# A two-block transformer forward pass on one core: the first transfers reordered, the first sum of squares taken by products with ones, idle products added, two small operations moved

## The chip, the core and the metric

The kernel runs on one core of one Trainium2 chip. The core has a matrix engine (TensorE, PE in the profile, with its weight loads listed as PEld), a vector engine (VectorE, DVE), a scalar engine (ScalarE, ACT), GpSimd (POOL) and SyncE (SP), which here issues all transfers; 16 DMA engines carry them. The metric is the device time of one execution in microseconds, as the median of several runs.

## The reference, cut to what matters

Two transformer blocks follow each other on 256 tokens of width 1024, all in fp32. What the change touches stands at the very start of the first:

```python
c_act = jax.nn.silu(c)
mod = c_act @ mod_w[layer] + mod_b[layer]
sh1, sc1, g1, sh2, sc2, g2 = jnp.split(mod, N_MOD, axis=-1)
u = modulate(rms_norm(h, norm_mix[layer]), sh1, sc1)   # x * (1 + scale) + shift
q, z_f, v, g = jnp.split(u @ a_w_in, ...)              # HGRN2 mixer, then gate, FFN
sm = softmax(a_lb, axis=0); lower_bounds = cumsum(sm, axis=0) - sm[0]
f = lb + (1 - lb) * sigmoid(z_f); k = (1 - lb) * (1 - sigmoid(z_f))
```

Behind that come the recurrence, a feed-forward layer, a banded attention layer with its own feed-forward layer, and the second block: sliding-window attention beside spatial gating, cross attention to a memory, and a mixture of 32 experts.

## The kernel before, in words

Activations are kept transposed: 1024 features as 8 chunks (k) of 128 partitions, 256 tokens along the free dimension; `h` holds the input. A matrix product in fp32 quality is done by three products in a faster format: each operand is split into a high part (`whi`, `uh`, made by ScalarE) and a remainder (`wlo`, `ul`, made by VectorE), and `mm3` (L197 to L200) issues high x high, high x low and low x high.

The start runs as follows. SyncE issues `crow` (the condition vector, 4 KB), the input `h` in four parts of 256 KB, and `cols` (107.5 KB: gains, biases and other column constants). ScalarE squares the four parts (L356), VectorE adds the squares to `sqs` (L358), and one pair of products with a matrix of ones (L486) sums over the partitions. `inv_rms` (L287 to L296) turns that sum into `r`: a logarithm and an identity on ScalarE, an exponential, and three operations on VectorE. Meanwhile `crow` is spread over the partitions by two products with ones (L362) and passed through silu into `cb`.

The modulation of the first norm is taken chunk by chunk, in `u_row(k)` (L500). Two tiles of 128 x 1024 modulation weights are each multiplied with `cb` and summed along the row by VectorE in `mod_row` (L368): g = 0 gives the shift, g = 1 the scale. Two small ScalarE operations (L512, L513) put bias and gain to them, VectorE makes `ut` from `h`, the scale and `r` (L516), ScalarE the high part `uh` (L517), VectorE the remainder `ul` (L521). `gb` (L490) is a product of `cols` columns that L513 reads. `w_split` (L524) splits a 128 x 512 piece of the weights `a_w_in`. The loop at L537 goes over 32 pieces, four for each chunk k; each step first issues, by the letters of `ROW_SEQ`, the next steps of `u_row(k + 1)` (r) and of the split three pieces ahead (s), then 12 matmuls: 48 for each chunk, in 8 chunks.

After that loop come the sigmoids of the forget gate (`f_out`, L582), operations with the lower bound (`lbt`, `lb`, `omlb`, `nomlb`; L552 to L562) and the next weights, split at L193 and L194.

What sets the order: the engines run their own queues in order. The order within a queue is chosen at build time by a planner that goes by data and by its own estimates; it may move an instruction ahead of others. `keep(...)` (tc.keep_in_program_order) pins an instruction behind the one that stands before it in the program on its engine. So in both kernels the first `mod_row` is pinned behind `gb`, and each `keep` after it behind the last one. Transfers are issued in the order of the program as far as their buffers are free: the weight buffers (`wslot`, tag "w") are six, the buffers of `whi` and `wlo` four each. `table()` loads the table set of logarithm and exponential on ScalarE; other sets are loaded where an operation needs one that isn't there.

Of the kernel before, what the change touches and what calls it, by code (L numbers as in the profile page):

```python
# [93 lines left out]
def _build(ctx, tc, nc, A, out, dbg):  # L94
# [20 lines left out]
    nc.sync.dma_start(crow, A["rows"][:, ROWS["c"][0]:ROWS["c"][0] + D])  # L115
    for i in range(4):
        nc.sync.dma_start(h[:, 2 * i:2 * i + 2, :], A["xT"][i * 256:i * 256 + 256].rearrange("(k p) t -> p k t", p=P))
    cols = cp.tile([P, NCOL], F32, name="cols")
    nc.sync.dma_start(cols, A["cols"])
    ident = cp.tile([P, P], F32, name="ident")  # L120
# [16 lines left out]
    def colblk(name):  # L137
        o, w = COLS[name]
        return cols[:, o:o + w]
# [17 lines left out]
    def uid(s):  # L157
        ctr[0] += 1
        return f"{s}{ctr[0]}"
# [188 lines left out]
    def hpair(kk):  # L348
        return h[:, 2 * kk:2 * kk + 2, :]
# [3 lines left out]
    sqs = gp.tile([P, 2, T], F32, tag="sq", name="sqs", bufs=2)  # L353
    for kk in range(4):
        sq = gp.tile([P, 2, T], F32, tag="whi", name=uid("sq"), bufs=4) if kk else sqs
        nc.scalar.activation(sq, hpair(kk), AF.Square)  # L356
        if kk:
            nc.vector.tensor_add(sqs, sqs, sq)  # L358
    cb = sp.tile([P, D], F32, name="cb")
    for i in range(2):  # L360
        ps = bank(pa).rearrange("p a b -> p (a b)")
        nc.tensor.matmul(ps, ones[0:1, :], crow[:, i * 512:i * 512 + 512], start=True, stop=True)  # L362
        nc.scalar.activation(cb[:, i * 512:i * 512 + 512], ps, AF.Silu)
# [119 lines left out]
    table()  # L483
    ss = pm.tile([P, T], F32, tag="mm", name=uid("ss"))
    for k2 in range(2):
        nc.tensor.matmul(ss, ones, sqs[:, k2, :], start=k2 == 0, stop=k2 == 1)  # L486
    r = inv_rms(ss, D)
# [8 lines left out]
    keep = tc.keep_in_program_order  # L496
# [3 lines left out]
    def u_row(k):  # L500

        wm = wslot(D)
        for g in range(2):
            nc.sync.dma_start(wm[:, g, :], A["modT"][g, k * P:k * P + P, :])
        ws[k] = wslot(2048)
        nc.sync.dma_start(ws[k][:, 0, :], A["a_w_in"][k * P:k * P + P, 0:2048])
        one = slice(k, k + 1)
        mod_row(wm[:, 0, :], 0, k, keep)
        yield
        mod_row(wm[:, 1, :], 1, k, keep)  # L510
# [39 lines left out]
    with tc.tile_pool(name="hgrn", bufs=1, reuse_waits="tile") as hp:  # L550

        lbt = hp.tile([P, 3, 8], F32, name="lbt")  # L552
        nc.vector.tensor_sub(lbt[:, 0, :], colblk("lb"), colblk("lb"))
# [1110 lines left out]
```

## Time and profile before

| | before |
|---|---|
| median of 3 runs | 1345.49 us (1344.38 to 1346.59) |
| the profiled execution | 1346.06 us, span 1344.3 us |
| TensorE busy | 1221.1 us (91%) |
| VectorE busy | 719.2 us (54%) |
| ScalarE busy | 571.6 us (43%) |
| GpSimd busy | 12.1 us (1%) |
| DMA | 80.9% of the 16 engines' span, 302 GB/s of HBM traffic |

The span is the time between the first and the last thing that the profile shows; the execution's own time is 1.76 us more. A busy share is an average over the whole span, and stages differ: the dense part fills TensorE and VectorE, the mixture of experts at the end waits for its weights.

### The profile page before, as it was taken

Reading aid. Unit: us, or ns where it says so; the run is one execution under the profiler, and the core shown is the slowest. Engines: PE = TensorE matmul, PEld = TensorE weight load, DVE = VectorE, ACT = ScalarE, POOL = GpSimd, SP = SyncE. Lnnn points to the kernel's source line nnn. Section 1 sums busy time; section 2 is a strip of 40 time slices with the busy share of each in tenths; the row PEclk is TensorE's granted clock in tenths of the full one; section 3 lists DMA queues with packets and bytes.
Section 4 is the critical chain, followed back from the end, with each engine's and each line's share of the span. In section 5 each row is a group of like instructions: output and inputs, shape, how many; then the busy total and the mean of one; then the engine's idle time right before and its main releaser. Section 6 shows DMA issues by size and latency. Waiting matters only on the chain.

```text
span 1344.3 us, 23689 instructions
## 1 busy us (share of the span) xinstructions
PE 1221.1 (91%) x9336; PEld 934.7 (70%) x9336; DVE 719.2 (54%) x1549; ACT 571.6 (43%) x1179; POOL 12.1 (1%) x36
## 2 busy tenths in 40 slices
PE   7999899999999999999999989999778776778795
PEld 5967899999979789999999889974223132222222
DVE  7999899888798877555568877631000000000000
ACT  5755664555575656555567767531101011000100
POOL 2000000000000000000000000000000000000000
PEclk9999999999999999999999989999898899888899
DMA  9958799999979649555235246889999999999998
GB/s 364 382 185 307 260 339 325 329 318 354 331 253 326 215 162 298 199 184 185 93 110 189 95 162 233 318 321 421 421 421 421 421 421 421 421 420 422 417 409 274
DMA packets 152566, 408.13 MB, mean 304 GB/s; under 512 B 11265, under 2 KB 79105, under 8 KB 129922
## 3 DMA queue, kind: packets, MB, share of 16 engines
q1 hardware_dynamic: 152450, 406.56, 80.9%
q8 instruction: 75, 1.23, 0.4%
q14 instruction: 41, 0.34, 0.1%
HBM read 403.38 MB, written 3.15 MB: 302 GB/s over the span
## 4 chain that ended last, share of the span: by engine, by line
PE 54%; DMA 33%; DVE 8%; ACT 2%; SPq 1%; issue 1%; POOL 0%; DVEq 0%; ACTq 0%
DMA w<-in_w 30%; PE acc L200 9%; PE acc L199 9%; PE acc L198 8%; PE ps L200 7%; PE ps L199 7%; PE ps L198 7%; DVE wlo L194 2%; DMA mt<-in_modT 1%; DVE mt L368 1%; PE ss L324 1%; PE r L1450 1%; DVE ut L335 1%; DMA w<-in_ffn_w_in 1%; SPq L1437 1%
## 5 line engine op out<-in xcount | busy, mean ns | idle before, releaser
L193 ACT ACTIVATE whi<-w 128x512 fp32r<-128x512 f32 (+1 forms) x448 | 278.5, 627 | 237.8 <-PE ps L199 110.0
L194 DVE TENSOR_TENSOR wlo<-w,whi 128x512 fp32r<-128x512 f32 (+1 forms) x448 | 299.8, 682 | 110.7 <-ACT whi L193 109.9
L1450 PE MATMUL r<-w,xe 128*32 128x512 f32 x1024 | 186.9, 664 | 58.8 <-DMA w<-in_w 58.6
L200 PE MATMUL ps<-uh,wlo 128*128 128x256 f32 x768 | 215.6, 281 | 1.3 <-DVE wlo L194 1.3
L199 PE MATMUL ps<-ul,whi 128*128 128x256 f32 x768 | 215.7, 281 | 0.5 <-DVE ul L342 0.5
L198 PE MATMUL ps<-uh,whi 128*128 128x256 f32 x768 | 215.6, 281 | 0.0
L1467 DVE SCALAR_TENSOR_TENSOR hs<-r,sc,hs 128x512 f32<-128x512 f32 (+1 forms) x9 | 6.1, 690 | 349.3 <-PE r L1450 348.9
L198 PE MATMUL acc<-uh,whi 128*128 128x256 f32 x592 | 168.7, 291 | 7.8 <-ACT uh L517 4.3
L1450 PEld LDWEIGHTS r<-w,xe 128*32 128x32 f32 x1024 | 39.6, 118 | 193.9 <-DMA w<-in_w 121.7
L200 PE MATMUL acc<-uh,wlo 128*128 128x256 f32 x592 | 167.5, 286 | 1.7 <-DVE wlo L194 1.7
L199 PE MATMUL acc<-ul,whi 128*128 128x256 f32 x592 | 168.2, 286 | 0.2 <-DVE ul L339 0.2
L200 PEld LDWEIGHTS ps<-uh,wlo 128*128 128x128 f32 x768 | 144.5, 188 | 2.1 <-DVE wlo L194 2.1
L199 PEld LDWEIGHTS ps<-ul,whi 128*128 128x128 f32 x768 | 144.6, 188 | 0.7 <-DVE ul L342 0.7
L198 PEld LDWEIGHTS ps<-uh,whi 128*128 128x128 f32 x768 | 144.6, 188 | 0.0
L368 DVE SCALAR_TENSOR_TENSOR mt<-mt,cb 128x1024 f32<-128x1024 f32 x96 | 116.8, 1219 | 11.7 <-DMA mt<-in_modT 11.7
L1496 PE MATMUL r<-w,hT 128*32 128x512 f32 (+1 forms) x544 | 94.3, 626 | 31.6 <-DMA w<-in_w 31.5
L198 PEld LDWEIGHTS acc<-uh,whi 128*128 128x128 f32 x592 | 111.8, 192 | 11.9 <-ACT uh L517 5.3
L200 PEld LDWEIGHTS acc<-uh,wlo 128*128 128x128 f32 x592 | 113.2, 192 | 3.3 <-DVE wlo L194 2.3
L199 PEld LDWEIGHTS acc<-ul,whi 128*128 128x128 f32 x592 | 113.3, 191 | 1.8 <-issue 0.8
L200 PE MATMUL acc<-hh,wlo 128*128 128x256 f32 x352 | 98.3, 279 | 0.3 <-DVE wlo L194 0.3
L198 PE MATMUL acc<-hh,whi 128*128 128x256 f32 x352 | 98.6, 280 | 0.0
L199 PE MATMUL acc<-hl,whi 128*128 128x256 f32 x352 | 98.2, 279 | 0.0
(327 smaller groups left out, 1699.8 us busy)
## 6 DMA issues: line engine op xcount, KB each, us to landing
w<-in_w SPq DMA_DIRECT2D x172, 1024.0 KB, 19.8
mt<-in_modT SPq DMA_DIRECT2D x96, 512.0 KB, 5.5
w<-in_ffn_w_in SPq DMA_DIRECT2D x88, 512.0 KB, 5.7
w<-in_ffn_w_out SPq DMA_DIRECT2D x22, 1024.0 KB, 8.5
w<-in_w SPq DMA_DIRECT2D x40, 512.0 KB, 10.2
w<-in_a_w_in SPq DMA_DIRECT2D x16, 1024.0 KB, 9.1
w<-in_modT SPq DMA_DIRECT2D x16, 512.0 KB, 8.8
w<-in_kv_w SPq DMA_DIRECT2D x8, 1024.0 KB, 6.9
```

The lines of the kernel that those rows point to most:

```text
L193: keep(nc.scalar.activation(hi, raw, AF.Copy))
L194: keep(nc.vector.tensor_sub(lo, raw, hi.bitcast(F32)))
L198: nc.tensor.matmul(o, lh, rh, start=first, stop=False, skip_group_check=True)
L199: nc.tensor.matmul(o, lh, rl, start=False, stop=False, skip_group_check=True)
L200: nc.tensor.matmul(o, ll, rh, start=False, stop=last, skip_group_check=True)
L324: nc.tensor.matmul(ss, ones, sq[:, k2, :], start=kk == min(adds, 1) and k2 == 0, stop=kk == 3 and k2 == 1)
L335: keep(nc.vector.scalar_tensor_tensor(t, src, gain, r, op0=ALU.mult, op1=ALU.mult))
L368: keep(nc.vector.scalar_tensor_tensor(w, w, 1.0, cb, op0=ALU.mult, op1=ALU.mult, accum_out=modr[:, g, j:j + 1]))
L1437: nc.sync.dma_start(ts[e][:, :, o % 512:o % 512 + o2 - o], src("w2", e)[:, o:o2].rearrange("(p c) n -> p c n", p=P))
L1450: keep(nc.tensor.matmul(hps[i][s, :], xe[k][:, s], w[nm, e, k], start=k == 0, stop=k == KC - 1))
L1467: nc.vector.scalar_tensor_tensor(hc[:, c, :], h3[:, c, :], rs, hc[:, c, :], op0=ALU.mult, op1=ALU.mult)
L1496: keep(nc.tensor.matmul(yp[s, :], hT[:, c, s], w[e, o // 512, c][:, o % 512:o % 512 + n], start=c == 0, stop=c == 3))
```

## The change

The first transfers are issued in another order: `crow`, two parts of `h`, the scale's modulation tile of chunk 0, the other two parts of `h`, the shift's tile, `cols`, and then the first row of `a_w_in` in two halves, the half that is split first ahead of the other. The tiles are allocated at the top; `u_row(0)` uses them instead of issuing its own transfers.

The squares are no longer added by VectorE. Each of the four parts is squared (three by VectorE, the last by ScalarE) and goes into the sum by two products with ones of its own. `inv_rms` is written out there with one ScalarE operation less. Between the parts stand idle products of ones with ones (2 at first, then 2, 2, 2 and 8), whose result nobody reads. The table load moves ahead of the last square. In each `u_row` the scale's row is now taken ahead of the shift's; the order of their transfers in the later chunks stays. The first operation of the lower bound is pinned behind what VectorE does before it in the program, that is, behind the last weight remainder of the loop.

```diff
     crow = sp.tile([P, D], F32, tag="mt", name="crow", bufs=3)[0:1]
     nc.sync.dma_start(crow, A["rows"][:, ROWS["c"][0]:ROWS["c"][0] + D])
+
+    wm0 = wp.tile([P, 2, D], F32, tag="w", name="wm0")
+    ws0 = wp.tile([P, 1, 2048], F32, tag="w", name="ws0")
     for i in range(4):
         nc.sync.dma_start(h[:, 2 * i:2 * i + 2, :], A["xT"][i * 256:i * 256 + 256].rearrange("(k p) t -> p k t", p=P))
+        if i % 2:
+            nc.sync.dma_start(wm0[:, 1 - i // 2, :], A["modT"][1 - i // 2, 0:P, :])
     cols = cp.tile([P, NCOL], F32, name="cols")
     nc.sync.dma_start(cols, A["cols"])
+    for i in (1, 0):
+        nc.sync.dma_start(ws0[:, 0, i * D:i * D + D], A["a_w_in"][0:P, i * D:i * D + D])
...
     table("silu_and_others")
-    sqs = gp.tile([P, 2, T], F32, tag="sq", name="sqs", bufs=2)
-    for kk in range(4):
-        sq = gp.tile([P, 2, T], F32, tag="whi", name=uid("sq"), bufs=4) if kk else sqs
-        nc.scalar.activation(sq, hpair(kk), AF.Square)
-        if kk:
-            nc.vector.tensor_add(sqs, sqs, sq)
+    keep = tc.keep_in_program_order
     cb = sp.tile([P, D], F32, name="cb")
+    ss0 = pm.tile([P, T], F32, tag="mm", name=uid("ss"))
+    idle = pb.tile([P, T], F32, tag="bg", name=uid("idle"))
+
+    def warm(n):
+
+        for _ in range(n):
+            keep(nc.tensor.matmul(idle[:, 0:P], ones, ones, start=True, stop=True))
+
+    def first_squares(kk, engine):
+        sq = gp.tile([P, 2, T], F32, tag="whi", name=uid("sq"), bufs=4)
+        if engine is nc.vector:
+            keep(nc.vector.tensor_mul(sq, hpair(kk), hpair(kk)))
+        else:
+            keep(nc.scalar.activation(sq, hpair(kk), AF.Square))
+        for k2 in range(2):
+            keep(nc.tensor.matmul(ss0, ones, sq[:, k2, :], start=kk == 0 and k2 == 0, stop=kk == 3 and k2 == 1))
+
+    warm(2)
     for i in range(2):
         ps = bank(pa).rearrange("p a b -> p (a b)")
-        nc.tensor.matmul(ps, ones[0:1, :], crow[:, i * 512:i * 512 + 512], start=True, stop=True)
-        nc.scalar.activation(cb[:, i * 512:i * 512 + 512], ps, AF.Silu)
+        keep(nc.tensor.matmul(ps, ones[0:1, :], crow[:, i * 512:i * 512 + 512], start=True, stop=True))
+        keep(nc.scalar.activation(cb[:, i * 512:i * 512 + 512], ps, AF.Silu))
+    table()
+    for kk in range(4):
+        first_squares(kk, nc.scalar if kk == 3 else nc.vector)
+        warm((2, 2, 2, 8)[kk])
...
-    table()
-    ss = pm.tile([P, T], F32, tag="mm", name=uid("ss"))
-    for k2 in range(2):
-        nc.tensor.matmul(ss, ones, sqs[:, k2, :], start=k2 == 0, stop=k2 == 1)
-    r = inv_rms(ss, D)
+
+    r, t = (gp.tile([P, T], F32, tag=f"rms_{x}256", name=uid(x), bufs=2 if x == "r" else 1) for x in "rt")
+    nc.scalar.activation(r, ss0, AF.Ln, scale=1.0 / D, bias=epsc[:, 0:1])
+    nc.scalar.activation(r, r, AF.Exp, scale=-0.5)
+    nc.vector.scalar_tensor_tensor(t, ss0, D * EPS, r, op0=ALU.add, op1=ALU.mult)
+    nc.vector.scalar_tensor_tensor(t, t, -0.5 / D, r, op0=ALU.mult, op1=ALU.mult)
+    nc.vector.scalar_tensor_tensor(r, t, 1.5, r, op0=ALU.add, op1=ALU.mult)
...
     def u_row(k):
 
-        wm = wslot(D)
-        for g in range(2):
-            nc.sync.dma_start(wm[:, g, :], A["modT"][g, k * P:k * P + P, :])
-        ws[k] = wslot(2048)
-        nc.sync.dma_start(ws[k][:, 0, :], A["a_w_in"][k * P:k * P + P, 0:2048])
+        if k:
+            wm = wslot(D)
+            for g in range(2):
+                nc.sync.dma_start(wm[:, g, :], A["modT"][g, k * P:k * P + P, :])
+            ws[k] = wslot(2048)
+            nc.sync.dma_start(ws[k][:, 0, :], A["a_w_in"][k * P:k * P + P, 0:2048])
+        else:
+            wm, ws[k] = wm0, ws0
         one = slice(k, k + 1)
+        mod_row(wm[:, 1, :], 1, k, keep)
+        yield
         mod_row(wm[:, 0, :], 0, k, keep)
-        yield
-        mod_row(wm[:, 1, :], 1, k, keep)
         yield
...
-        nc.vector.tensor_sub(lbt[:, 0, :], colblk("lb"), colblk("lb"))
+        keep(nc.vector.tensor_sub(lbt[:, 0, :], colblk("lb"), colblk("lb")))
```

## Rows read from the trace of the kernel before

**Rows 1.** Windows by stage: us, busy time and count of each engine, PEclk, DMA, GB/s

```profile
24.00:59.00 35.00, 34.91 (x295) 34.71 (x294) 34.18 (x61) 21.25 (x45) 0.00 (x0) 1.00 1.02 390
870.00:1344.00 474.00, 377.35 (x2235) 146.31 (x2233) 30.24 (x99) 52.62 (x131) 0.20 (x1) 0.93 0.98 400
```

**Rows 2.** Timeline of the start: start us, us, engine, line, operation, out<-in, count, [idle before]

```profile
2.28 3.75 PE L362 MATMUL acc<-crow,ones 1*128 1x512 f32 x4 [2.28 <-DMA crow<-in_rows]
...
9.38 0.16 DVE L490 SCALAR_TENSOR_TENSOR gb<-cols 128x8 f32<-128x8 f32 x1
...
9.52 2.07 PE L486 MATMUL ss<-sqs,ones 128*128 128x256 f32 x4 [3.50 <-DVE sqs L358]
...
9.71 1.22 DVE L368 SCALAR_TENSOR_TENSOR w<-w,cb 128x1024 f32<-128x1024 f32 x1
...
11.37 1.22 DVE L368 SCALAR_TENSOR_TENSOR w<-w,cb 128x1024 f32<-128x1024 f32 x1
...
13.48 0.63 ACT L530 ACTIVATE whi<-w 128x512 fp32r<-128x512 f32 x1 [0.19 <-DMA w<-in_a_w_in]
...
14.76 0.48 DVE L516 SCALAR_TENSOR_TENSOR ut<-h,modc,r 128x256 f32<-128x256 f32 x1
...
15.89 0.80 PE L198 MATMUL acc<-uh,whi 128*128 128x256 f32 x2 [4.29 <-ACT uh L517]
```

**Rows 3.** DMA issues at 2.66, 3.17, 3.68 and 4.16: count, KB each, us to landing

```profile
h<-in_xT SPq DMA_DIRECT2D x1, 256.0 KB, 5.3
...
cols<-in_cols SPq DMA_DIRECT2D x1, 107.5 KB, 5.1
...
w<-in_modT SPq DMA_DIRECT2D x1, 512.0 KB, 6.0
...
w<-in_modT SPq DMA_DIRECT2D x1, 512.0 KB, 6.8
```

**Rows 4.** Timeline of the first chunks of the loop, columns as in rows 2

```profile
17.01 0.41 PE L198 MATMUL acc<-uh,whi 128*128 128x256 f32 x1
17.22 0.41 PE L199 MATMUL acc<-ul,whi 128*128 128x256 f32 x1
...
21.01 0.28 PE L198 MATMUL ps<-uh,whi 128*128 128x256 f32 x1
21.12 0.28 PE L199 MATMUL ps<-ul,whi 128*128 128x256 f32 x1
...
21.63 0.28 ACT L512 ACTIVATE modc<-modr,cols 128x1 f32<-128x1 f32 x1
21.81 0.37 ACT L513 ACTIVATE modc<-modr,gb,cols 128x1 f32<-128x1 f32 x1
22.22 0.48 DVE L516 SCALAR_TENSOR_TENSOR ut<-h,modc,r 128x256 f32<-128x256 f32 x1 [1.04 <-ACT modc L513]
...
27.82 0.39 ACT L513 ACTIVATE modc<-modr,gb,cols 128x1 f32<-128x1 f32 x1 [0.24 <-DVE w L368]
28.30 0.48 DVE L516 SCALAR_TENSOR_TENSOR ut<-h,modc,r 128x256 f32<-128x256 f32 x1
```

**Rows 5.** Timeline where the loop ends and the forget gate begins

```profile
58.69 1.29 DVE L532 TENSOR_TENSOR wlo<-w,whi 128x512 fp32r<-128x512 f32 x2
59.20 1.28 ACT L582 ACT_TABLE_LOAD   x1
60.49 2.07 ACT L582 ACTIVATE f<-acc 128x512 f32<-128x512 f32 x4
...
63.39 0.68 DVE L194 TENSOR_TENSOR wlo<-w,whi 128x512 fp32r<-128x512 f32 x1
...
64.48 0.40 PE L199 MATMUL acc<-wlo,uh 128*128 128x512 f32 x1
```

**Rows 6.** Windows of 1 us in the mixture of experts, columns as in rows 1

```profile
948.00:949.00 1.00, 0.29 (x1) 0.14 (x2) 0.00 (x0) 0.00 (x0) 0.00 (x0) 1.00 1.01 418
949.00:950.00 1.00, 1.00 (x2) 0.00 (x0) 0.00 (x0) 0.00 (x0) 0.00 (x0) 0.54 1.06 442
```

More of the change, by code (lines that the diff above doesn't have):

```diff
@@ L495, in _build @@
     qps = [[bank(), bank()], [bank(), bank(pb)]]
-    keep = tc.keep_in_program_order
     ws = [None] * KC
```

## The prediction, made blind

> **What bounds the kernel now.** I read the stages first, then the start instruction by instruction, then the landings, then the loop that follows.
>
> The stages [rows 1] say what a saved microsecond is worth. From 24 to 59 us TensorE is busy 34.91 of 35 us and VectorE 34.18: both are full, and what starts earlier ends earlier. The last 474 us run at 400 GB/s with 0.98 of the DMA time used, but that stream can only begin when the dense part gives up its weight buffers. So I let a shift of the first rows reach the end undiminished; I see nothing after the start that waits for a fixed time.
>
> The start [rows 2] is a chain on VectorE. The small product `gb` runs at 9.38, after `cols` has landed; two modulation rows follow (9.71 and 11.37, 1.22 us each), then three operations for `r`, the first weight remainder and `ut` at 14.76; the first real matmul goes at 15.89. On ScalarE the first weight split stands at 13.48, after 0.19 us of waiting for its data. What set the chain going was the wire: counting its issue, `cols` landed at 3.17 + 5.1 = 8.27, modulation row 0 at 3.68 + 6.0 = 9.68 and row 1 at 4.16 + 6.8 = 10.96, and the last part of the input at 2.66 + 5.3 = 7.96 [rows 3].
>
> In the loop [rows 4] matmuls start 0.21 us apart at 17 us and 0.11 to 0.12 us apart at 21 us: 256 columns at 1.2 and at 2.4 GHz, although the granted clock prints 1.00. Some 20 matmuls from 15.89 on go at the slow level. That holds the split buffers, ScalarE waits, and VectorE sits idle 1.04 us before the second row's `ut` at 22.22.
>
> **The change, part by part.**
>
> *Transfers in another order.* The bytes are the same, so I read landings by position. Before, 1,028 KB were down at 7.96, 1,135 at 8.27, 1,647 at 9.68 and 2,159 at 10.96 [rows 3]. Now 512 KB of modulation come ahead of the third part of the input and 512 more ahead of `cols`. By interpolation the last input part (1,540 KB) lands at 9.4 instead of 8.0, the second modulation tile (2,052) at 10.7 and `cols` (2,159) at 11.0 instead of 8.3. SyncE issues these some 0.5 us apart, well ahead of the wire, so its queue costs nothing; the split weight transfer adds one issue, and the half needed first lands about 1.2 us earlier, which no row shows as the limit.
>
> *Where that hurts.* The first modulation row is kept behind `gb`, which reads `cols`. So although its own tile is there at about 8 us (1,028 KB), it can't start before about 11.1. Of the 1.66 us from one row's start to the next, about 0.5 were three small lower-bound operations, which are gone from here; the rows now take 1.15 + 1.22, from 11.1 to 13.5. From the end of the second row (11.37 + 1.22 = 12.59) to `ut` it was 2.17 us: two small operations, the split, the remainder, with the `r` operations beside them. Less the 0.19 for data that is 1.98, so `ut` at 15.4, 0.6 later than 14.76, and the three `r` operations fit beside it as before. The bounds: if `gb` is not late at all, the rows can begin at 9.7 and `ut` at 14.1, -0.7; if the `r` operations stand between the two modulation rows, +1.9 (rival three). I take +0.6, the sum in program order.
>
> *Squares into the sum.* Three additions of 0.69 on VectorE become three products of the same shape, and ScalarE loses three squares: nothing gained on VectorE. The sum is now eight fp32 products instead of two. The two at 9.52 took 2.07 us at the slow level [rows 2], about 0.86 each. TensorE is held by the `cb` products until 6.0 (2.28 + 3.75), then has 6 real and 6 idle products before the last pair. Each idle product is half as wide, 0.43. All slow, that is 5.2 + 2.6 = 7.8 us: the last pair starts at 13.8 and ends at 15.5, too late; all fast from 8 us on, the last pair waits for the last square (9.4 + 0.63) and ends near 11.3, 0.3 before the 11.59 of before. I expect 12 to 13. From the sum's end to `ut` it was 14.76 - 11.59 = 3.17 us, some of it the second modulation row and some the identity that is gone; a sum at 12.2 meets `ut` at 15.4 even at 3.17. So: 0, with bounds -0.3 and +2.0 (the sum at 15.5 and 2 us from there).
>
> *Idle products.* Up to 14 more of them, on an engine that is otherwise waiting, cost only by delaying the sum (counted). Their worth is the 1.04 us of VectorE idle time [rows 4], not the 2 us that 20 matmuls lose, because at 0.118 us TensorE would meet VectorE's chain: without the gap `ut` follows `ut` by 22.22 - 14.76 - 1.04 = 6.42. I take -1.0; bounds -2.0 (20 matmuls, 0.1 us each) and 0. The level can be lost again: at 949 us the granted clock, 1.00 until then, falls to 0.54 in a microsecond that follows one with TensorE busy only 0.29 us [rows 6], and here some 2 to 3 us lie between the last idle product and the first real one. The Trainium skill, "TensorE: Matmul & The Clock Gate" (HAM oscillation), says that an engine left idle goes back to the low rate and pays the slow start again; by it alone the gain here would be 0. The trace agrees that a sparse stretch loses the level; I leave it a one in ten rival.
>
> *Modulation rows swapped in every row.* In the loop ScalarE's two small operations come in the order L512, L513. Before, L512 was free early and only L513 waited for the second modulation row (0.24 us, at 27.82), ending 28.21; `ut` ran at 28.30 [rows 4]. Now L512 needs the second row too, and L513 follows it by 0.18 (21.63, 21.81): `ut` at about 28.43. VectorE has no slack, so +0.13 for each of rows 2 to 7 and 0.05 for row 1: +0.8. Bounds 0 (if VectorE had hidden waits to give) and +1.3 (7 times the 0.18).
>
> *The lower-bound chain moved.* `keep` puts its first subtraction behind the last remainder, which ends at 58.69 + 1.29 = 59.98 [rows 5]. ScalarE's exponential then comes at about 60.15 instead of 9.95. The table for the sigmoid is loaded at 59.20 now, while ScalarE waits for the accumulators. If the exponential goes first, that load starts at 60.35: 1.15 us later for the sigmoids at 60.49, the next weight split and its remainder on VectorE (63.39, ended 64.07). TensorE takes that remainder at 64.48, so 0.4 is hidden: +0.7. Bounds 0 and +2.4 (rival two).
>
> **Sum.** +0.6 + 0 - 1.0 + 0.8 + 0.7 = +1.1 us. The profiled execution took 1346.06 us (span 1344.3 and 1.76 around it), so its like would be 1347.2; it lies 0.6 above the median 1345.49, so I predict 1346.6.
>
> **Rivals.**
> 1. *It does what it is meant to.* `gb` isn't late and the first matmul goes 0.7 us earlier, the clock is high (-1.0 to -1.5), VectorE's swap is hidden and the exponential finds a gap: -0.7 - 1.2 = -1.9, 1343.6. For it: VectorE loses 0.5 us of small work at the start, and the 1.04 us gap is real. Against it: the landing of `cols`, and a VectorE that is full to 98% from 24 to 59.
> 2. *Slower: the exponential falls between the sigmoids.* The first sigmoid's accumulators are ready at about the time of the subtraction; if the queue has one sigmoid ahead of the exponential, ScalarE loads the exponential's table, then the sigmoid's again: 2 loads of 1.28 + 0.21 = 2.8 us, less the 0.4 hidden = 2.4 in place of 0.7. Total +2.8, 1348.3. It decides by the order on ScalarE alone. For it: the tie at 60 us; against it: the exponential comes first in the program. The Trainium skill, "ScalarE: Activation LUTs" (What ACT_TABLE_LOAD costs), adds a drain to each switch, 2.66 us in all; by that the total would be near +5.6. The trace shows the sigmoids starting 1.29 us after the load began, so the row decides.
> 3. *Slower at the start: `r` between the modulation rows.* Nothing but data orders `r` on VectorE, so it may stand ahead of the second row; the row then ends 1.3 later (1.9 - 0.6), and all behind it. Total +2.4, 1347.9. For it: `r` comes first in the program; against it: before, both rows ran ahead of `r`.
> 4. *The clock stays low or falls back.* The -1.0 is lost, which makes +2.1, and the sum of squares may come up to 2.0 later, +4.1; at +2.6, a quarter of the way, 1348.1.
>
> **Chances.** Forecast 0.42, rival one 0.22, two 0.16, three 0.10, four 0.10. A measurement of this kernel tells 0.2% (2.7 us) from no change, so faster means under 1342.8 and slower over 1348.2. Faster needs more than rival one in full, 0.06. Slower takes most of rival two, the unlucky parts of three and four, and the forecast's tail: 0.20. The same 0.74. The range reaches from a little beyond rival one to a microsecond above rival two, 1343.3 to 1349.4.
>
> **What would show it.** `gb` and the first modulation row at about 11 us and `ut` at 15.4 (right), or the modulation row at 8 to 9 us (transfers wrongly read). The first real matmuls 0.12 us apart, and `ut` to `ut` 6.4 to 6.5 us after the first row. L513 ending 0.13 closer to its `ut` in each later row, and `ut` to `ut` longer by as much. One or three table loads near 60 us. The prediction is wrong if the product at 64.48 comes more than 1 us earlier or 3 us later, or if a shift there is not found again at the end.

## The result, and the profile after

The changed kernel took 1365.64 us (median of 4 runs, 1365.24 to 1368.59), the kernel before beside it 1345.86 us: a ratio of 1.0143, 95% interval [1.0128, 1.0158], 17 to 21 us slower. The forecast was 1346.6 us, with a range up to 1349.4. The prediction was wrong in size and in kind.

The profiled execution has a span of 1366.6 us, 22.3 more than before. Where the time goes is read by following the same instruction through both traces. The table gives, for each kernel of this study, how many microseconds later than in the profiled kernel before an instruction starts, at seven places (their start times before in the head), and the span's difference. The rows below "after" belong to the experiments, which are told further down.

| kernel | 15.9 first real matmul | 57.1 last `ut` of the loop | 70.3 last `qx` product | 94.8 last `uml` | 148.4 last `ul` of the HGRN output | 205.6 first FFN output product | 450.3 first `kT,qT` product | span |
|---|---|---|---|---|---|---|---|---|
| after | +3.6 | +4.6 | +7.5 | +7.5 | +7.2 | +14.8 | +22.5 | +22.3 |
| e1 pin alone | -0.6 | -1.1 | +1.8 | +3.4 | +5.3 | +14.5 | +18.3 | +17.2 |
| e5 table loads alone | +0.1 | -0.2 | +2.4 | +4.5 | +2.6 | +9.3 | +15.1 | +14.2 |
| e6 pin, no exponential | -0.5 | -0.3 | +1.4 | +1.1 | +0.9 | +9.4 | +15.1 | +15.3 |
| e11 third order | -0.5 | -1.1 | +0.4 | +1.2 | +3.7 | +3.6 | +5.3 | +5.5 |
| e2 no pin | +3.0 | +4.0 | +4.0 | +4.0 | +4.1 | +3.3 | +3.6 | +5.2 |
| e3 no pin, no idle products | +2.1 | +2.5 | +2.5 | +2.5 | +3.8 | +3.9 | +3.4 | +2.4 |
| e9 e3 with r behind the rows | +0.8 | +1.1 | +1.1 | +1.1 | +2.4 | +2.7 | +4.2 | +4.0 |
| e4 swap alone | +1.1 | +2.0 | +2.0 | +2.0 | +1.6 | +2.6 | +1.6 | +2.6 |
| e13 transfers alone | +0.8 | +1.0 | +1.0 | +1.0 | +1.3 | +1.5 | +2.0 | +2.4 |
| e14 squares alone | +2.0 | +1.8 | +1.8 | +1.8 | +1.7 | +2.1 | +1.3 | +0.3 |
| e15 14 idle products alone | +0.6 | -0.5 | -0.4 | -0.5 | +1.8 | +2.1 | +1.9 | +0.9 |
| e10 26 idle products alone | +2.7 | +0.5 | +0.5 | +0.5 | +1.9 | +3.0 | +2.3 | +2.2 |
| e12 start mended | +2.5 | +0.3 | +0.3 | +0.3 | +0.5 | +1.2 | +2.6 | +6.1 |
| e7 rows' transfers by GpSimd | +0.2 | +0.4 | +2.0 | +1.7 | +5.7 | +12.8 | +37.2 | +36.9 |
| e8 the same with the pin | +0.1 | +0.1 | +4.5 | +4.5 | +8.3 | +14.9 | +38.8 | +39.0 |

Three cautions. The start itself moves by a few tenths to 1 us from run to run (e11 changes nothing there and shows -0.5 and -1.1). And each trace is one execution, while the kernel before ranged over 7 to 8 us in a set of runs (its medians there 1347.0 to 1347.8): differences of 1 or 2 us late in the span are spread, and totals are taken from the ratios. The profiled execution of after is the slowest of its four, 3 us above the median; those of e2 and e12 lie 2.6 and 3.0 us above theirs, those of e14, e8 and e11 3.9, 3.4 and 2.3 below. Last, TensorE's granted clock isn't the same in every execution: between 92 and 102 us it is 0.83 in e3, e9, e10 and e11 and 1.00 in before, e13 and e15. In e3, e9 and e10, which change nothing there, that stretch lies in the 1.3 to 1.4 us that they lose between 94.8 and 148.4.

The line "after" has three losses: +3.6 us at the start (+4.6 by the loop's end), +2.9 at the sigmoids, and +15 between 95 and 450 us; from there on it is 1 to 1. First the start, from the timeline of after (start, duration, engine, line, operation; in brackets the idle time before it and what ended it); it answers to [rows 2].

```profile
10.69 0.16 DVE L516 SCALAR_TENSOR_TENSOR gb<-cols 128x8 f32<-128x8 f32 x1
10.77 1.22 DVE L392 SCALAR_TENSOR_TENSOR wm<-wm,cb 128x1024 f32<-128x1024 f32 x1
...
12.95 1.03 PE L377 MATMUL ss<-sq,ones 128*128 128x256 f32 x4
13.82 1.95 PE L368 MATMUL idle<-ones 128*128 128x128 f32 x16
...
14.59 0.42 ACT L510 ACTIVATE r<-r 128x256 f32<-128x256 f32 x1
15.04 0.42 DVE L511 SCALAR_TENSOR_TENSOR t<-ss,r 128x256 f32<-128x256 f32 x1 [3.04 <-ACT r L510]
15.38 1.22 DVE L392 SCALAR_TENSOR_TENSOR wm<-wm,cb 128x1024 f32<-128x1024 f32 x1
...
18.37 0.48 DVE L544 SCALAR_TENSOR_TENSOR ut<-h,modc,r 128x256 f32<-128x256 f32 x1
...
19.50 0.80 PE L205 MATMUL acc<-uh,whi 128*128 128x256 f32 x2 [3.74 <-ACT uh L545]
...
25.53 0.34 PE L205 MATMUL ps<-uh,whi 128*128 128x256 f32 x1
```

`gb` and the first modulation row start at 10.7 to 10.8, a little ahead of where the prediction had them. Then VectorE's queue has `t`, the first of r's operations, ahead of the second row: it waits 3.04 us for the exponential, which waits for the sum of squares (ended at 13.98), and a row that could have run from 12 us on, its tile having landed at 10.2, starts at 15.38. The last idle product ends at 15.77, TensorE is idle for 3.74 us, and the real matmuls start 0.21 us apart until 25.5, as at 17 us in [rows 4]. The window of that stretch (columns as in [rows 1]) shows the granted clock at 0.50:

```profile
19.50:25.50 6.00, 6.00 (x27) 5.98 (x28) 5.26 (x9) 2.73 (x6) 0.00 (x0) 0.50 0.98 364
```

Then the sigmoids (timeline of after, ScalarE), which answer to [rows 5]:

```profile
63.80 1.28 ACT L610 ACT_TABLE_LOAD   x1
65.10 0.60 ACT L610 ACTIVATE f<-acc 128x512 f32<-128x512 f32 x1
65.71 1.28 ACT L582 ACT_TABLE_LOAD   x1
67.01 0.21 ACT L582 ACTIVATE lbt<-lbt 128x8 f32<-128x8 f32 x1
67.23 1.28 ACT L610 ACT_TABLE_LOAD   x1
68.53 1.57 ACT L610 ACTIVATE f<-acc 128x512 f32<-128x512 f32 x3
```

One sigmoid stands ahead of the exponential: three table loads where there was one, as rival two had it, 1.28 + 0.21 + 1.28 and small gaps = 2.8 us on ScalarE.

The rest comes from a place that the change doesn't touch. Put side by side by tile and operation, at least 22 of SyncE's 562 transfers and 92 of VectorE's 1,549 instructions stand elsewhere in their queues than before, all but 4 and 13 of them behind the start. (The expectations below count every entry that is displaced, and so have larger numbers.) This is one spot of many, first before, then after: where the residual (`h`, L405 before and L429 after), the modulation rows (`mt`) and the remainder that TensorE needs next (`wlo<-fw`) meet.

```profile
171.87 0.42 DVE L194 TENSOR_TENSOR wlo<-fw,whi 128x256 fp32r<-128x256 f32 x1
...
173.21 1.65 DVE L405 SCALAR_TENSOR_TENSOR h<-acc,modc,h 128x256 f32<-128x256 f32 x4
...
174.78 1.21 DVE L368 SCALAR_TENSOR_TENSOR mt<-mt,cb 128x1024 f32<-128x1024 f32 x1
174.80 1.13 PE L324 MATMUL ss<-sq,ones 128*128 128x256 f32 x4 [0.27 <-ACT sq L310]
...
179.47 0.42 DVE L295 SCALAR_TENSOR_TENSOR r<-t,r 128x256 f32<-128x256 f32 x1
```

```profile
175.49 1.22 DVE L392 SCALAR_TENSOR_TENSOR mt<-mt,cb 128x1024 f32<-128x1024 f32 x1
...
178.81 1.23 DVE L392 SCALAR_TENSOR_TENSOR mt<-mt,cb 128x1024 f32<-128x1024 f32 x1 [1.50 <-DMA mt<-in_modT]
180.09 1.23 DVE L392 SCALAR_TENSOR_TENSOR mt<-mt,cb 128x1024 f32<-128x1024 f32 x1
181.24 1.66 DVE L429 SCALAR_TENSOR_TENSOR h<-acc,modc,h 128x256 f32<-128x256 f32 x4
...
183.56 0.42 DVE L201 TENSOR_TENSOR wlo<-fw,whi 128x256 fp32r<-128x256 f32 x1
...
184.04 0.58 PE L206 MATMUL ps<-wlo,umh 128*128 128x256 f32 x1 [4.45 <-DVE wlo L201]
184.85 4.47 PE L331 MATMUL ss<-sq,ones 128*128 128x256 f32 x10
...
191.88 0.42 DVE L302 SCALAR_TENSOR_TENSOR r<-t,r 128x256 f32<-128x256 f32 x1
```

Before, that `wlo` and then the last four residuals go ahead of the next row. After, two rows stand in front of the residuals, the first waits 1.50 us for its tile, and behind both wait not only the residuals but the `wlo` that TensorE needs next: it idles for 4.45 us. The windows of after (TensorE, weight loads, VectorE, ScalarE, GpSimd busy, granted clock, DMA share, GB/s) show what that costs on top:

```profile
180.00:185.00 5.00, 0.96 (x4) 0.96 (x5) 4.96 (x16) 0.63 (x1) 0.00 (x0) 0.77 1.04 390
185.00:190.00 5.00, 5.00 (x17) 4.10 (x16) 0.32 (x1) 1.28 (x3) 0.00 (x0) 0.55 1.10 363
```

Behind the idle stretch the granted clock is 0.55, the sum of squares runs slowly, and r's chain, 6.0 us late at the residual's start at 168.61 (162.65 before), is 12.4 us late at 191.88 (179.47 before). So one stretch gives 6.5 us. The other half of the 15 us comes between 206 and 450 us, in the FFN and behind it, where no single wait of TensorE is longer than 1.0 us; of 200 us from 210 on TensorE is busy 198.38 before (first line) and 194.39 after (second).

```profile
210.00:410.00 200.00, 198.38 (x1560) 191.54 (x1560) 175.47 (x318) 110.74 (x188) 0.44 (x3) 1.00 0.90 319
```

```profile
210.00:410.00 200.00, 194.39 (x1571) 188.31 (x1571) 169.90 (x304) 103.01 (x176) 0.43 (x3) 1.00 0.90 316
```

### The profile page after: what moved, and what is told of

It reads as the page before. It is cut to its first block, busy times and chain, and to the rows that moved or that the text cites. A ratio compares the mean times of both kernels' runs of the same rounds, so it can differ in the third digit from the quotient of the medians.

```text
span 1366.6 us, 23772 instructions
## 1 busy us (share of the span) xinstructions
PE 1236.2 (90%) x9380; PEld 947.1 (69%) x9380; DVE 720.8 (53%) x1549; ACT 571.9 (42%) x1177; POOL 12.0 (1%) x36
## 4 chain that ended last, share of the span: by engine, by line
PE 52%; DMA 34%; DVE 8%; ACT 3%; issue 2%; SPq 1%; POOL 0%; DVEq 0%; ACTq 0%; POOLq 0%
DMA w<-in_w 30%; PE acc L207 8%; PE acc L206 8%; PE acc L205 8%; PE ps L207 6%; PE ps L206 6%; PE ps L205 6%; DMA mt<-in_modT 4%; DVE wlo L201 2%; PE ss L331 1%; DVE mt L392 1%; PE r L1478 1%; PE acc L261 1%; DVE ut L342 1%; SPq L1465 1%
## 5 line engine op out<-in xcount | busy, mean ns | idle before, releaser
L1478 PE MATMUL r<-w,xe 128*32 128x512 f32 x1024 | 183.8, 657 | 56.3 <-DMA w<-in_w 56.3
## 6 DMA issues: line engine op xcount, KB each, us to landing
w<-in_w SPq DMA_DIRECT2D x40, 512.0 KB, 10.2
```

The costliest lines, as they stand in the source:

```text
L1478: keep(nc.tensor.matmul(hps[i][s, :], xe[k][:, s], w[nm, e, k], start=k == 0, stop=k == KC - 1))
```

## The experiments

Two theories stood against each other at first. A: the pin on `lbt` makes the planner choose another order for the work behind it. B: the later start shifts transfers against each other, and the pin costs its table loads alone.

**e1, the pin alone**

```diff
-        nc.vector.tensor_sub(lbt[:, 0, :], colblk("lb"), colblk("lb"))
+        keep(nc.vector.tensor_sub(lbt[:, 0, :], colblk("lb"), colblk("lb")))
```

> The kernel before, with one thing of the change: the subtraction of lbt keeps its place in program order (L553 of before). Its later order of instructions is the change's from the HGRN stage on, its start is the old one. Theory A (the pin makes the planner order the later work otherwise): the loss that the trace of after collects behind 60 us comes with it, +2.9 us at the sigmoids (an exponential among them, two extra table loads) and some +15 us between 100 and 400 us: about 1363 us (1360 to 1366), and the first modulation row after the HGRN stage runs near 85 us and not near 102. Theory B (the later losses come from the later start, which shifts transfers against each other): only the table loads, +2.9 us: about 1348.5 us.

1362.08 us, ratio 1.0108 [1.0084, 1.0132]. One `keep` on a 128x8 subtraction costs 11 to 18 us. The first modulation row behind the loop runs at 80.9 (102.06 before), and 18 transfers and 79 vector instructions stand elsewhere, as many as in after behind its start. Theory A holds, B falls.

**e2, everything but the pin, and e3, without the idle products too**

```diff
-        keep(nc.vector.tensor_sub(lbt[:, 0, :], colblk("lb"), colblk("lb")))
+        nc.vector.tensor_sub(lbt[:, 0, :], colblk("lb"), colblk("lb"))
-        warm((2, 2, 2, 8)[kk])     # and warm(2): only in e3
```

> The changed kernel without the pin on lbt; everything else of the change stands, and the later order is that of the kernel before. Theory A: only the start's loss is left, +3.6 us where the first u row is shifted (ut at 18.37 for 14.76) and up to +4.6 by row 7: 1349 to 1350.5 us, one table load at the sigmoids, modulation row near 105 us. Theory B: the late losses stay, 1362 us or more; the table loads' 2.9 us go.

> The changed kernel without the pin and without the idle products (16 matmuls of 128 columns less at the start). If the idle products do what they are put there for, the pairs of the squares' sum take 2.08 us for two records again and not 1.03, Ln starts up to 1 us later and the whole is about 1 us longer than without the pin alone (1350 to 1351.5). Rival: VectorE's squares or the Exp behind Ln set the end, TensorE has slack: within 0.4 us of it. In both the real matmuls begin 0.21 us apart, since TensorE stood idle over 3 us before them.

1348.94 us, 1.0011 [0.9998, 1.0024], and 1349.78 us, 1.0024 [1.0012, 1.0035]; their own ranges overlap. With the pin goes nearly the whole loss, and behind the start no transfer and no vector instruction of either stands elsewhere than before.

The start of the three kernels shows what the idle products did. In each, TensorE works back to back from 6.0 us to the end of the sum of squares, the exponential and `t` wait for that end, and `ut` follows it by the same 4.39 us:

| | e3, no idle products | e2 | after |
|---|---|---|---|
| last square starts | 8.77 | 9.57 | 8.95 |
| sum of squares ends | 12.52 | 13.40 | 13.98 |
| `ut` starts | 16.91 | 17.79 | 18.37 |

```profile
12.37 1.03 PE L377 MATMUL ss<-sq,ones 128*128 128x256 f32 x4
...
14.45 0.42 DVE L511 SCALAR_TENSOR_TENSOR t<-ss,r 128x256 f32<-128x256 f32 x1 [1.84 <-ACT r L510]
```

(Timeline of e2.) So the idle products among the parts lengthened the queue at whose end the sum stands, by 0.9 us in e2 and 1.5 in after. `cols`, 0.8 us later in e2 than in e3, isn't the reason: VectorE had done the first row and waited 1.84 us for the exponential (1.78 in e3). The real matmuls reach the high level after 3.9 us in e3 (21.9) and after 5.6 in e2 (24.5). That can't be laid on the idle products, because in the twelve kernels without them this slow stretch lasts anything from 3.4 us (e11) to 5.6 (e4, e6), with 4.7 in before.

The two traces that follow are a warning. VectorE's idle time ahead of modulation rows (us, times), first after, then e2:

```profile
  DMA mt<-in_modT: 26.3, 22
```

```profile
  DMA mt<-in_modT: 24.1, 19
```

Before it was 11.7. So e2 has nearly all of VectorE's waiting for modulation tiles and almost nothing of the loss: this sum, which looks like the cause, isn't it. What the spot above suggests instead is the place in the queue, whether TensorE's next operand stands behind the row that waits; that was not tried by itself.

**e4, the swap alone**

> The kernel before, with one thing of the change: in each u row the scale's modulation row goes first and the shift's second. The later order is that of before. By the prediction's term, +0.13 us for a row from the scale operation that waits no longer but for the shift's that now does, 0.8 us in all: 1346.3 us. Rival: the two operations behind a row are exchanged without a cost, since VectorE's own sum of 2.1 us a row sets the pace: within 0.3 us of before.

1348.83 us, 1.001 [0.9996, 1.0023]. From the second `ut` to the last, each step is 0.11 to 0.13 us longer than before, 0.74 in all, in e4 as in after, e2, e3 and e9: the forecast's term. The first step's 0.2 more is found in e6 too, whose slow stretch of TensorE is as long as e4's and whose rows aren't swapped. The +1.1 at the start is e4's own: its first row reads the tile that is issued second (landed at 10.67, the other at 9.41) and starts at 10.79, 9.71 before. The changed kernel issues that tile first.

**e5, two table loads alone, and e6, the pin without its loads.** e1 leaves open whether the pinned chain, the loads or the new order costs. These take them apart.

```diff
             nc.scalar.activation(f[:, h0:h0 + 2, :], ps[i], AF.Sigmoid)
+            if hf == 0 and i == 0:
+                table()                                    # e5
-        nc.scalar.activation(lbt[:, 1, :], lbt[:, 0, :], AF.Exp)
+        nc.scalar.activation(lbt[:, 1, :], lbt[:, 0, :], AF.Identity, bias=ones[:, 0:1])   # e6, with the pin
```

> The kernel before with no instruction of lbt moved: only a load of the exponential's table is put between the first and the second sigmoid (and with it the sigmoid's table is loaded again): two loads more, near 60 us. The transfers' order is, instruction for instruction, that of the pin alone. Theory A' (what costs is the later order that the planner chooses when its estimate of the time near 60 us shifts, whatever shifts it): +2.9 us there and some +12 us between 100 and 400 us, 1359 to 1363 us, TensorE waiting about 4.5 us for a wlo near 184 us. Theory C (the pinned chain itself, six operations on VectorE, costs the rest): only the two loads, about 1349 us.

> The pin alone again, with the exponential of lbt (of a zero) replaced by an identity plus one: ScalarE loads no extra table, one load at the sigmoids as before. The transfers' order is the pin's but for two. Theory A': the +2.9 us at 60 us goes and the +12 us between 100 and 400 us stays: 1358 to 1360 us. Theory D (the two loads near 60 us start the whole: what comes later is only their delay, met again by transfers): about 1347 us.

e5: 1361.01 us, 1.0099 [1.0081, 1.0116]. e6: 1360.67 us, 1.0088 [1.0072, 1.0105]. Neither the pin nor the loads are needed: each alone brings the pin's order of transfers (e6 but for one), VectorE's order but for some 12 instructions, and nearly the same loss. In e6 ScalarE has no extra load,

```profile
60.23 0.60 ACT L582 ACTIVATE f<-acc 128x512 f32<-128x512 f32 x1
60.72 0.29 ACT L554 ACTIVATE lbt<-lbt,ones 128x8 f32<-128x8 f32 x1
60.91 1.56 ACT L582 ACTIVATE f<-acc 128x512 f32<-128x512 f32 x3
```

and at 148 us it is only 0.9 late; but in its waits of TensorE from 150 to 210 us (engine, line, released by, us in total, times, longest) the long one is there,

```profile
PE ps L199 <- DVE wlo L194: 4.3, 1, 4.3
```

where the longest of before is this:

```profile
PE acc L200 <- DVE wlo L194: 0.6, 1, 0.6
```

It is there in e1 (4.6) and e5 (3.7) as well, and in e2 TensorE's longest wait in that window is 1.2. Theories C and D fall. What the kernels with the loss share is the order, and two different edits near 60 us each set it off; that they do so through the planner's estimates of time is the reading that fits, not something a trace shows. The loads' own price stays open. At 70 us, counted from the last `ut`, e1 loses 2.9 us, e5 (loads alone) 2.7, and e6 (no extra load) still 1.7, with the pinned chain's five small operations on VectorE ahead of `kd` (61.04 to 62.05). Between the ratios of e1 and e6 (1.0108 and 1.0088) lie 2.7 us, which their intervals don't tell apart.

**e7 and e8, modulation transfers issued by GpSimd**, to take them out of SyncE's queue.

```diff
-            nc.sync.dma_start(w, A["modT"][g, j * P:(j + 1) * P, :])
+            nc.gpsimd.dma_start(w, A["modT"][g, j * P:(j + 1) * P, :])
```

> The kernel before with the 96 modulation transfers (mt) issued by GpSimd and not by SyncE, so that none stands in SyncE's queue behind a weight transfer that waits for its buffer (the planner's order changes with it, on all engines). If that queue is what makes the rows late, VectorE's wait for mt falls from 11.7 us to a few and the kernel gains up to 8 us: 1338 to 1345. Rival: the rows wait for their three buffers and the wire; VectorE's wait stays near 12 us or grows, and the time stays within 5 us of 1347.

> The same (modulation transfers issued by GpSimd) with the pin on lbt. If the pin's loss behind 100 us comes from modulation transfers held up in SyncE's queue, it isn't there now: only +2.9 us from the table loads over the same kernel without the pin. Rival: the order of the rows on VectorE's queue costs by itself: +10 us or more over the same kernel without the pin.

1384.30 us, 1.0267 [1.0246, 1.0289], and 1388.87 us, 1.0306 [1.0289, 1.0323]. Both expectations for e7 missed. The rows wait 31.8 us for their tiles, not a few, and TensorE is busy 183.56 us of the 200 from 210 on (198.38 before). GpSimd is busy 33.40 us there, nearly all of it with issues, 0.53 us each. With the pin it is 4.6 us more, not 15. That agrees with a loss that hangs on the order (e7 and e8 differ in one of SyncE's transfers and some 40 vector instructions, and e8 has the two extra table loads), but both carry another order than all else here, so I don't call it shown. Nor does any run part GpSimd's issuing from that other order.

**e11, a third order**

```diff
             nc.scalar.activation(f[:, h0:h0 + 2, :], ps[i], AF.Sigmoid)
+            if hf == 1 and i == 0:
+                nc.scalar.activation(lbt[:, 0, :], f[:, h0, 0:8], AF.Exp)
```

> The kernel before with an exponential behind the third sigmoid call (first of the second half), so one table load more near 70 us and none between the sigmoids of the first half. The planner answers with a third order, near neither of the two: 24 of SyncE's entries moved against before (79 for the pin). If a shift of the planner's estimate costs by the order it happens to choose, this is anywhere from +1.5 us (the load alone, about 1349) to +15; if any order but the old one is bad, +10 us or more; if the pin's loss belonged to the place at 60 us and not to the order, about 1349.

1353.89 us, 1.0049 [1.0034, 1.0063]: 4.6 to 8.5 us, of which one load is 1.3. By the count used above, 12 transfers and 56 vector instructions stand elsewhere. So not every other order costs 12 us, and this one isn't free.

**e13 and e14, the transfers and the squares alone.** The start's terms one by one, on the kernel before: e13 takes the diff's first part and `wm0`, `ws0` in `u_row`; e14 takes `first_squares` and the written-out r.

> The kernel before with the first transfers in the change's order and nothing else of it (the shift's row still first). The prediction's term: cols lands near 11 us for 8.3, gb and the first modulation row wait for it, and ut goes 0.6 us later (15.4 for 14.76); here with the old sum of squares, the last part of the input at 9.4 for 8.0 also moves the sum, by up to 1.4 us: +0.6 to +1.5 us in all. Rival: the transfers' order is free, since the two modulation rows stand back to back now (11.1 to 13.5): ut within 0.3 us of before.

> The kernel before with the direct sum of squares (eight products, three squares on VectorE, r written out) and nothing else: old transfers, no swap, no pin, no idle products. The prediction's term: 0, with bounds -0.3 and +2.0. From the runs so far the sum ends at 12.0 to 12.5 us when TensorE has all eight products to do behind 6.0, against 11.59 before, and the planner puts t between the two modulation rows, so the second row waits for the exponential: ut near 16.5 for 14.76, +1.5 to +2 us. Rival: with the old transfers the squares come a microsecond earlier and the sum with them, +0.5 or less.

e13: 1348.40 us, 1.001 [0.9997, 1.0022]. e14: 1350.22 us, 1.0026 [1.0013, 1.0039]. From the timeline of e13:

```profile
10.60 0.16 DVE L496 SCALAR_TENSOR_TENSOR gb<-cols 128x8 f32<-128x8 f32 x1
10.68 1.22 DVE L374 SCALAR_TENSOR_TENSOR wm<-wm,cb 128x1024 f32<-128x1024 f32 x1
...
11.82 1.22 DVE L374 SCALAR_TENSOR_TENSOR wm<-wm,cb 128x1024 f32<-128x1024 f32 x1
...
15.55 0.48 DVE L525 SCALAR_TENSOR_TENSOR ut<-h,modc,r 128x256 f32<-128x256 f32 x1
```

Late rows back to back, `ut` 0.8 later: the term of +0.6. And of e14:

```profile
5.96 6.61 PE L371 MATMUL ss<-sq,ones 128*128 128x256 f32 x16
...
13.62 0.42 DVE L503 SCALAR_TENSOR_TENSOR t<-ss,r 128x256 f32<-128x256 f32 x1 [0.97 <-ACT r L502]
13.96 1.22 DVE L384 SCALAR_TENSOR_TENSOR w<-w,cb 128x1024 f32<-128x1024 f32 x1
...
16.77 0.48 DVE L533 SCALAR_TENSOR_TENSOR ut<-h,modc,r 128x256 f32<-128x256 f32 x1
```

Eight products fill TensorE from 5.96 to 12.57, one microsecond past the end of before, though the last square was done at 8.6; and `t` stands between the rows. `ut` is 2.0 us late. The ratio is worth 1.8 to 5.3 us, although the profiled execution, the fastest of its twelve, ends only 0.3 us late.

**e9, r behind both rows** (e3 with the three operations of r kept behind the second row)

> The changed kernel without the pin on lbt, without the idle products, and with the three vector operations of r pinned behind the second modulation row of chunk 0 (before that t stood between the two rows and waited for the exponential). The sum of squares ends at about 12.5 us as it did there, so r is ready at about 14.8. If t between the rows is what makes the start late, the second row runs from about 11.8 (13.91 there), ut at 15.0 to 15.4 (16.91 there): 1.5 us less than the same kernel without this, 1346.5 to 1348.5 us. Rival: the sum of squares on TensorE is what is late, r ends the wait anyway and ut gains under 0.5 us.

1349.93 us, 1.002 [1.0009, 1.0031]. The second row starts at 12.59 and not 13.91, `ut` at 15.60 and not 16.91: 1.3 us, a little under the forecast. At 95 us that is still 1.3 us less than e3, but the ratios of the two don't tell them apart.

**e10, e15 and e12, idle products up to the first real matmul**

```diff
     r = inv_rms(ss, D)
+    idle = pb.tile([P, T], F32, tag="bg", name=uid("idle"))
+    for _ in range(26):     # 14 in e15
+        tc.keep_in_program_order(nc.tensor.matmul(idle[:, 0:P], ones, ones, start=True, stop=True))
```

> The kernel before with 26 idle products (128 columns) behind its sum of squares, so that TensorE is busy until close to the first real matmul; nothing else moves, all other queues have before's order. If the clock then stays high, the first real matmuls start 0.12 us apart, VectorE's idle time of 1.04 us before the second row's ut goes, and all behind it comes 1.0 us earlier: the -1.0 of the prediction's sum, about 1346.5 us. Rival: the matmuls still start 0.21 us apart for a while, nothing is gained (1347.5), or the idle products reach past 15.9 us and cost up to 1 us.

> The kernel before with 14 idle products behind its sum of squares. With 26 of them they ran from 10.83 to 18.5 us, the first real matmul went 2.7 us late and then at 0.12 us; 0.5 us of that was left at 64 us. Fourteen should end at about 15.9, when the first real matmul is due. If the prediction's term is right, the matmuls start 0.12 us apart at once, VectorE's gap before the second row's ut goes and the product at 64 us comes 1.0 us earlier (up to 2): 0.999 of before. Rival: the high level isn't held, or VectorE has another wait in the gap's place: no change at 64 us.

> What the runs point to, put together: the changed kernel without the pin and the swap, cols issued ahead of the modulation tiles, r's vector operations behind the second row, and 28 idle products behind the sum of squares in place of the sixteen among its parts. Later order as before. The sum of squares ends near 12.5 us and ut comes near 15 us, as before (14.76); if the idle products keep the clock, 1.0 us is won behind it: 1345 to 1347 us. Rival: the sum on TensorE, one microsecond later than before (11.59), takes that back: 1347.5 to 1349.

e10: 1346.88 us, 0.9995 [0.9982, 1.0008]. e15: 1345.88 us, 0.999 [0.9978, 1.0002]. e12: 1349.22 us, 1.0014 [1.0003, 1.0025]. In e10 the idle products ran until 18.8 us and held the first real matmul back by 2.7 us; from there to 57 us 2.2 us were won back. In e15 their number fits:

```profile
11.40 4.44 PE L490 MATMUL idle<-ones 128*128 128x128 f32 x28
...
15.40 0.48 DVE L519 SCALAR_TENSOR_TENSOR ut<-h,modc,r 128x256 f32<-128x256 f32 x1
...
16.53 0.50 PE L198 MATMUL acc<-uh,whi 128*128 128x256 f32 x2 [0.69 <-ACT uh L520]
...
17.39 0.28 PE L198 MATMUL acc<-uh,whi 128*128 128x256 f32 x1
17.51 0.28 PE L199 MATMUL acc<-ul,whi 128*128 128x256 f32 x1
```

The matmuls start 0.12 us apart from 17.3 on, and the step from the first `ut` to the second is 6.35 us for 7.46 before: 1.1 us won, the 1.0 of the prediction (in the other kernels without idle products and swap that step is 6.85 to 7.67, longest where the slow stretch is). The shift goes from +0.6 (the modulation tiles landed 0.6 later in that execution) to -0.5 by the loop's end. But it isn't kept. At 105 us it is gone, and then a row waits for its tile that didn't wait before (first before, then e15):

```profile
112.61 1.23 DVE L368 SCALAR_TENSOR_TENSOR mt<-mt,cb 128x1024 f32<-128x1024 f32 x1
```

```profile
114.60 1.22 DVE L368 SCALAR_TENSOR_TENSOR mt<-mt,cb 128x1024 f32<-128x1024 f32 x1 [1.95 <-DMA mt<-in_modT]
```

The order on SyncE, VectorE and ScalarE is before's, to the last instruction. The time can't be told from before's. In e12, 28 idle products were again too many (the first real matmul +2.5 us, +0.3 at 57), and its total isn't better than before. No version here beats the kernel before by more than the measurement can tell; e15 comes nearest.

## Why the prediction was wrong

- *"I let a shift of the first rows reach the end undiminished; I see nothing after the start that waits for a fixed time."* This step failed, and with it the forecast. I priced each edit where it stands, and held the work behind it fixed. The planner orders that work anew, and one pin near 60 us moved 18 transfers and 79 vector instructions (e1), and TensorE then waited 4.6 us (4.45 in after) for a remainder that had stood ahead of the rows before. In the runs that is worth 9.7 to 14.2 us without any extra load (e6) and 11.3 to 17.8 with them (e1), of a loss of 17 to 21. The sign that I had set showed: the first product with a remainder behind the loop, at 64.48 before, went at 71.63. And without any new order the step fails too, though by little: in the nine kernels that keep before's order behind the start (e2, e3, e4, e9, e10, e12 to e15), shifts of -0.5 to +4.0 us at 57 us are +1.3 to +4.2 at 450. Rows behind the start do wait for their tiles (11.7 us in all before), and in some executions the clock falls there.
- *"so 0.4 is hidden: +0.7. Bounds 0 and +2.4 (rival two)."* (the lower-bound chain). Rival two came about in full, +2.9 us at the sigmoids, with nothing hidden. I gave it 0.16 as a tie; the queue decided for it. Its ceiling, priced on ScalarE alone, was the wrong kind of bound: e6, without the loads, is 1.7 us late there by VectorE's small operations, and what the chain's place did to the order isn't in it at all.
- *"I take +0.6, the sum in program order."* Right for the transfers and `gb`: +0.8 alone (e13), `gb` at 10.7 where 11.0 to 11.1 was reckoned.
- *"So: 0, with bounds -0.3 and +2.0"* (squares). The upper bound was the value, +2.0 (e14), but not for the reason given, a sum that ends at 15.5. The eight products held TensorE to 12.6, within the 12 to 13 that I expected. But I took it that r still fits behind both rows, 3.17 us from the sum's end to `ut`; the planner put `t` between them (as it did in e4, with the old r), and it was 4.39. That is rival three, which I priced at +1.3 beyond the forecast and gave 0.10; e9, without it, gains just that. In the changed kernel it met a later sum, at 13.98.
- *"I take -1.0"* (idle products). The worth was right, the premise wrong. 1.1 us is what a kept clock gives by the second `ut` (e15). But the change's idle products end 3.74 us before the first real matmul, and the real ones ran slowly for 6 us. Rival four named this; that "some 2 to 3 us lie between" should have made it the forecast. And TensorE was not "otherwise waiting": between 6.0 and 13.98 us it never was, so they cost 1.5 us against e3, where the prediction had their delay "(counted)" in a sum at 12 to 13.
- *"+0.13 for each of rows 2 to 7"* (swap, +0.8). Right: 0.11 to 0.13 a row, 0.74 in all (e4); the ratio alone doesn't show it.

By the sum of start terms the changed kernel without the pin would be some 3 to 4 us late in the traces (+4.0 in e2), against ratios worth +1.5 and +3.2 us in e2 and e3; the range reached to +3.9 over the median of before. The start alone would by these ratios have left the result inside it, though not by the forecast's own sum: its terms of 0 and -1.0 were wrong. What remains open: which of the moved rows make up the 4 to 8 us between 206 and 450 us. It wasn't tried to force one part of the order and leave the rest, nor a fourth modulation buffer.

## What to carry to other kernels

Where a planner orders the queues, compare the orders of both kernels to their ends before pricing an edit: a pin on an operation that costs 0.16 us moved work far behind it, at some 12 us (e6). Read a wait by what stands behind it in the queue and not by its sum: 24 us of waiting for modulation tiles cost next to nothing in one order, and in another a stretch with one such wait of 1.50 us lost 6.5. Idle products are worth their time only if they last until the real work begins and don't stand in the queue ahead of products that others wait for; count them from the trace's own durations. And don't read a cause out of one pair of traces where the same quantity, here the length of the slow stretch, differs as much between kernels without the edit.

## What the runs showed of the hardware

- An idle gap of 0.69 us between the last idle product and the real work kept TensorE's high level (e15: matmuls 0.12 us apart, 2.4 GHz); one of 3.74 us lost it (after: 0.21 us apart, 1.2 GHz, granted clock 0.50, until 25.5). The Trainium skill, "TensorE: Matmul & The Clock Gate" (HAM oscillation), says that an engine left idle goes back to the low rate; these two rows agree.
- The slow stretch at the start of the real work differs from kernel to kernel, and nothing that was changed explains it: 3.4 us (e11) to 5.6 (e4, e6) in twelve kernels without idle products, 4.7 in before, 5.6 and 6 in e2 and after.
- The granted clock can differ between kernels that do the same work: between 92 and 102 us it is 0.83 in e3, e9 and e10, and 1.00 in before, e13 and e15. No run explains that.
- A single stall of 4.45 us in mid-kernel was followed by 5 us at a granted clock of 0.55, and one of 4.63 in e1, ended at 183.57, goes with 0.56 from 182 to 188 us: such a wait of TensorE costs more than itself.
- Loading a table between sigmoids costs 1.28 us each time and the next operation follows within 0.03 us, at all three places in after.
- GpSimd spends 0.53 us on each 512 KB transfer that it issues (e7, 96 of them).
